# Attention's products with the values in plain float32, two groups of heads side by side in TensorE's column halves, and a seldom-run expert loop moved from the first pair of experts to the last

## The chip, the cores and the metric

One core of a Trainium2 chip runs the whole program. The metric is device time in microseconds (us), from the start to the end of one execution. The engines are TensorE (PE in the profile; its weight loads are PEld), VectorE (DVE), ScalarE (ACT), GpSimd (POOL) and SyncE (SP, which here issues nearly all transfers).

## The reference

512 tokens of width 1024 pass two blocks. The first block is one layer: a mixer of two attentions, then a mixture of experts. The second block is two layers of differential attention beside a Fourier mix, each followed by a SwiGLU.

```
# block 1, mixer: 8 heads of 64; "D" is top-k attention with one shared key/value head,
# "S", "W", "C" are selected, windowed and compressed attention with 2 key/value heads (4 query heads each)
p = masked_softmax(s, mask)
o = einsum('bthk,btkd->bthd', p, vs)
o_b = gc * o_cmp + gs * o_slc + gw * o_win
# block 1, experts: 32 experts, each token goes to 2 of them
y = (silu(gate) * up) @ w_down[e]
# block 2, per layer: 8 heads, values 64 wide, two score maps a head
p = softmax(s, axis=-1)
a = p[:, :, 0] - lam * p[:, :, 1]
o = einsum('bhqk,bkhd->bqhd', a, v)
```

All of it is float32.

## The kernel before

**Number formats.** Nearly every product of float32 matrices is made from three products of type float32r, a one-pass format with a shorter mantissa: each operand is split in a rounded high part and a low rest (`split`: a copy on ScalarE or VectorE, then a subtraction, usually on VectorE), and `mm3` adds high by high, high by low and low by high. The products of attention weights and values are made in another way. The values stand as a stationary tile of 128 columns, 64 of the high part and 64 of the low part (`VS` and `Vc` in block 1, `vs` in block 2); the attention weights `e` are split in `ph` and `pl`; two float32r matmuls of 512 columns then put the result of the high values into rows 0 to 63 of the bank `po` and that of the low values into rows 64 to 127. When a bank is complete, ScalarE copies its lower half (`pt`, `pot`) and VectorE adds the two halves (`o`, `op`).

The experts' products are plain float32: `up` and `down` work on a pair of experts, 64 slots each, and the two experts' results go to rows 0 to 63 and 64 to 127 of a bank, so that each matmul uses 64 of the array's 128 columns.

**Order of the work.** The program order on TensorE is made by generators. `weave` runs a chain (the attention's phases) against a fill (projections that do not depend on it) by a running estimate of TensorE's time, `self.pe`, which `mm` advances. `after` and `later` put work off by so many microseconds of that estimate. The instructions then pass the framework's scheduler, which may reorder an engine's instructions inside a stretch without branches.

**Block 1** (`attend1`). Units of work are a kind (S, W, C, then D) and one of four query blocks `i`. For each, `q_part` makes the sums of the softmax, `b_part` turns their logarithms into two more rows of the query operand, and `k_part` makes the scores again, transposed, with keys in the partitions, takes the exponential (`e`) and issues the products with the values. `k_part` goes over two groups of four heads `g`, and in each over the key blocks `j`. Each (g, j) puts one entry on the list `pend`; an entry is issued when more than four wait (`late`), or between the heads of the next `q_part`. There are 68 such entries: 20 for each of S, W and D, 8 for C.

**Block 2** (`mixer2`). `pv_phase` does the same for a pair of heads `j`: over the two heads `hd`, and in each over four key blocks `kt`, two score maps and exponentials `e0`, `e1`, their combination on VectorE, the split in `ph` and `pl`, and an entry on `pend`. There are 32 entries a layer. When a head pair is complete, `norm` follows, put off by `after`.

**Experts** (`experts`). A loop over pairs `p` of experts: `up`, `mid`, then for the pair before it `turn`, `down` and `scatter` (an add into the tokens' rows in memory by an indirect DMA). `chunk(c)` gathers the tokens of two pairs. The weights come in 192 units of 512 KB, which `fetch` requests when a buffer is freed; 31 buffers hold them. `rest_of_rows` serves the tokens of an expert beyond its 64 slots in a loop of dynamic length, `tc.For_i(0, n, 1)`, for which every engine loads the count `nblk` and all engines meet. With these inputs no expert has more than 64 tokens and the loop's body does not run. In the kernel before it stands in the pair p = 0:

```
            if not p:
                rest_of_rows()
            if prev:
                A = turn(prev[0], 128)
```

Of the kernel before, what the change touches and what calls it, by code (L numbers as in the profile page):

```python
# [32 lines left out]
T = 512  # L33
D = 1024
# [70 lines left out]
class Kernel:  # L105
# [374 lines left out]
    def mixer1(self, hT):  # L480
# [13 lines left out]
        VS = pers.tile([128, NT, 5, 128], F32R, name="VS")  # L494
# [13 lines left out]
        Vc = pers.tile([128, 2, 128], F32R, name="Vc")  # L508
        for z in (KAc, KCc, Vc):
            nc.vector.memset(z.bitcast(F32), 0.0)  # L510
# [138 lines left out]
        def proj_tok():  # L649

            raw = b1.tile([128, KT, 352], F32, name="vraw")
            hi = b1.tile([128, KT, 352], F32R, name="vhi")
            lo = b1.tile([128, KT, 352], F32R, tag="kraw", name="vlo")
            wv = w.rearrange("(k p) n -> p k n", p=128)
            for c, n, m in ((0, "va", 64), (64, "v_slc", 128), (192, "v_win", 128), (320, "wi", 8), (328, "gb", 24)):
                a = slice(c, c + m)
                nc.sync.dma_start(raw[:, :, a], wv[:, :, W_IN[n]:W_IN[n] + m])
                self.split(hi[:, :, a], lo[:, :, a], raw[:, :, a])
            for t in range(NT):
                ps = self.bank()  # L660
# [12 lines left out]
            nc.vector.scalar_tensor_tensor(e, lng, -1.0, lng, op0=OP.mult, op1=OP.max)  # L673
            nc.scalar.activation(e, e, AF.Exp, scale=-1.0)
            nc.vector.tensor_scalar(e, e, 1.0, None, op0=OP.add)
            le = b1.tile([128, NT, 24], F32, name="lgl")
            self.log(b1, le, e, "lgn")
            nc.vector.scalar_tensor_tensor(lng, lng, 0.0, le, op0=OP.min, op1=OP.subtract)
            bclose()
            self.mark("tok")  # L680

        def compress():
# [48 lines left out]
            for which in "kv":  # L731
# [28 lines left out]
                else:  # L760
# [3 lines left out]
                    nc.scalar.activation(Vc[0:31, :, 0:64], p, AF.Copy)  # L764
                    nc.vector.tensor_sub(Vc[0:31, :, 64:128], p, Vc[0:31, :, 0:64].bitcast(F32))
# [73 lines left out]
    def attend1(self, hT, DR, B, top_k, rt):  # L839
# [106 lines left out]
        def k_part(kind, i):  # L946
# [4 lines left out]
            for g in range(2):  # L951
                if first:
                    out[g] = self.bank("po")
                gs = slice(4 * g, 4 * g + 4)
                v = {"D": 0, "S": 1 + g, "W": 3 + g, "C": g}[kind]
                nj = 1 if kind == "C" else i + 1
                def pv(j, ph, pl, po=out[g], g=g, v=v):
                    st = B["Vc"][:, g] if kind == "C" else VS[:, j, v]
                    self.mm(po, st, ph, first and j == 0, False)
                    self.mm(po, st, pl, False, last and j == nj - 1)  # L960
                    if not last or j < nj - 1:
                        return
                    t = ap.tile([64, T], F32, tag="pt", name="pt")
                    nc.scalar.activation(t, po[64:128], AF.Copy)
                    o = ap.tile([128, 2, 128], F32, tag="o", name="o", bufs=2)
                    for r in range(2):
                        pick = lambda x: x.rearrange("p (a r t) -> p a r t", a=2, r=2)[:, :, r]
                        nc.vector.tensor_add(o[r * 64:(r + 1) * 64], pick(po[:64]), pick(t))
                    d = DR["oa" if kind == "D" else "ob"]
# [3 lines left out]
                for j in range(nj):  # L973
                    o = self.bank()
                    qa = QA[:, gs].rearrange("p h t -> p (h t)")
                    qb = QB[0:66, gs].rearrange("p h t -> p (h t)")
                    if kind == "C":
                        ka, kc = B["KAc"][:, g], B["KCc"][0:66, g]
                        mk = B["cmk"][:, i:i + 1].to_broadcast([128, 4, 128])
                    else:  # L980
                        js = slice(j * 128, (j + 1) * 128)
                        ka, kc = KA[:, v, js], KC[0:66, v, js]
                        mk = None
# [8 lines left out]
                    e = ap.tile([128, T], F32, tag="e", name="e", bufs=TUNE["ee"])  # L992
                    nc.scalar.activation(e, o, AF.Exp)
                    ph = ap.tile([128, T], F32R, tag="ph", name="ph", bufs=TUNE["eb"])
                    pl = ap.tile([128, T], F32R, tag="pl", name="pl", bufs=TUNE["eb"])
# [432 lines left out]
    def experts(self, R):  # L1428
# [133 lines left out]
        def rest_of_rows():  # L1562

            Xs, Y = (wp.tile([128, n], F32, name="rest", tag=f"rest{n}", bufs=1) for n in (KT * 64, D))
            wp.tile([128, 32], F32, name="gap", bufs=1)
# [4 lines left out]
            with tc.For_i(0, n, 1):  # L1570
# [15 lines left out]
                def unit(kind, k):  # L1586
                    raw = wp.tile([128, D], F32, tag="Y", name="Y", bufs=1)
# [11 lines left out]
        wp, wclose = self.pool("mw", 2, gap=104)  # L1599
# [16 lines left out]
        for p in range(17):  # L1616
# [205 lines left out]
    def mixer2(self, l, hT):  # L1822
# [35 lines left out]
        stacks, b8s, ops, puts, pend, tails = {}, {}, {}, [], [], []  # L1858

# [88 lines left out]
        def pv_phase(j):  # L1948
# [4 lines left out]
            def pv(po, hd, kt, ph, pl):  # L1953
                v = vs[:, kt, 2 * j + hd]
                self.mm(po, v, ph, kt == 0, False)
                self.mm(po, v, pl, False, kt == NT - 1)
                if kt == NT - 1:
                    if hd == 0:
                        while tails:
                            self.now(tails.pop(0))  # L1960
                        ops[j] = vp.tile([128, T], F32, tag="op", name="op", bufs=1)
                    t = vp.tile([128, T], F32, tag="po", name="pot", bufs=1)[:64]
                    nc.scalar.activation(t, po[64:128], AF.Copy)
                    nc.vector.tensor_add(ops[j][hd * 64:(hd + 1) * 64], po[:64], t)
                    if hd:
                        sq = vp.tile([128, T], F32, tag="sq", name="sq", bufs=1)
                        nc.scalar.activation(sq, ops[j], AF.Square)
                        tails.append(self.after(TUNE["sq"], lambda: norm(j, ops.pop(j), sq)))

            for hd in range(2):  # L1970
                po = self.bank("po")
                for kt in range(NT):
                    kk = slice(kt * 128, (kt + 1) * 128)
                    p = []
                    for c in range(2):
# [4 lines left out]
                        e = vp.tile([128, T], F32, tag=f"e{c}", name="e", bufs=TUNE["e2"])  # L1980
# [3 lines left out]
                    ph, pl = (vp.tile([128, T], F32R, tag=n, name=n, bufs=TUNE["p2"]) for n in ("ph", "pl"))  # L1984
                    self.split(ph, pl, p[0], (nc.scalar, nc.vector)[kt % 2], nc.gpsimd if kt % 2 < TUNE["pp"] else None)
                    pend.append(lambda a=(po, hd, kt, ph, pl): pv(*a))
                    yield
                    if len(pend) > TUNE["late2"]:
# [3 lines left out]
        def norm(j, op, sq):  # L1992
# [3 lines left out]
            v, c = (vp.tile([128, T], F32, tag=n, name=n, bufs=TUNE["e2"]) for n in ("e0", "e1"))  # L1996
# [14 lines left out]
        def proj_v(ws):  # L2011
# [11 lines left out]
            for t in range(NT):  # L2023
                p = ps[t].rearrange("p (h d) -> p h d", h=NH2)
                nc.scalar.activation(vs[:, t, :, 0:64], p, AF.Copy)
                nc.vector.tensor_sub(vs[:, t, :, 64:128], p, vs[:, t, :, 0:64].bitcast(F32))
# [64 lines left out]
        vs = vp.tile([128, NT, NH2, 128], F32R, name="vs", bufs=1)  # L2091
# [121 lines left out]
```

## Time and profile before

| | |
|---|---|
| median of 3 runs (lowest, highest) | 2066.06 us (2063.63, 2068.55) |
| the profiled execution, its own time | 2063.88 us |
| its span, first to last instruction | 2062.1 us |
| mean granted TensorE clock | 0.973 of full speed |
| busy in the span | PE 94%, PEld 74%, DVE 55%, ACT 41%, POOL 11% |

The stages, in us from the span's start: block 1's projections to about 190, its attention to about 430, merge and router to about 537, the experts to about 805; block 2's first layer has its attention from about 880 to 1050 and its SwiGLU until 1430, the second layer its attention from about 1490 to 1665. A busy time counts a matmul from start to modelled end, and matmuls overlap, so the spacing of their starts tells what one costs. In the window view each engine has its busy time and, in brackets, its number of instructions; PEclk is the granted clock (0.50 is 1.2 GHz, 1.00 is 2.4 GHz, a value between them a mixture of the two).

### The profile page before, as it was taken

How to read it: one execution, taken by the hardware profiler on the slowest of the kernel's cores; microseconds unless marked ns; L12 is line 12 of the kernel's file. 1: busy time of each engine (PE TensorE's matmuls, PEld its weight loads, DVE VectorE, ACT ScalarE, POOL GpSimd, SP SyncE). 2: the span in 40 equal slices, each digit the busy share in tenths (PEclk: the TensorE clock that was granted, in tenths of full speed). 3: DMA queues.
4: the chain of work that ended last, by engine and by line, in shares of the span. 5: the costliest groups of instructions: out<-in, count | busy, mean ns of one | idle time of the engine just before them, and what ended most of it. 6: DMA issues, size and time to landing. Idle time of an engine off the chain costs nothing.

```text
span 2062.1 us, 25783 instructions
## 1 busy us (share of the span) xinstructions
PE 1938.5 (94%) x9430; PEld 1519.1 (74%) x9430; DVE 1128.8 (55%) x2038; ACT 844.1 (41%) x1619; POOL 223.6 (11%) x186
## 2 busy tenths in 40 slices
PE   7689999999799999899999999999899999999998
PEld 6567778778555444777778888888687778888886
DVE  7687997654521213587884333234587983333234
ACT  5354656733212113576733323222476833323220
POOL 3143111033000101101010000001001010000001
PEclk9899999999899999999999999999999999999999
DMA  6666433377699996734424333433844335333332
GB/s 178 150 170 154 113 87 98 110 218 272 251 375 396 396 388 202 206 95 128 121 99 126 92 102 92 160 95 101 196 111 131 112 122 152 95 98 96 116 99 72
DMA packets 284496, 328.69 MB, mean 159 GB/s; under 512 B 25562, under 2 KB 206842, under 8 KB 284112
## 3 DMA queue, kind: packets, MB, share of 16 engines
q1 hardware_dynamic: 276912, 306.54, 47.7%
q0 software_dynamic: 7456, 20.49, 3.8%
q8 instruction: 75, 1.23, 0.2%
q14 instruction: 53, 0.43, 0.1%
HBM read 286.63 MB, written 43.38 MB: 160 GB/s over the span
## 4 chain that ended last, share of the span: by engine, by line
PE 49%; DVE 4%; DMA 3%; ACT 2%; issue 1%; SPq 0%; POOL 0%; POOLq 0%; DVEq 0%; ACTq 0%
PE b L136 46%; PE po L136 3%; DVE nm L1917 1%; DMA wr<-in_w_in_dram 1%; DMA ks<-bnc 1%; ACT b L1918 1%; DMA wr<-in_c_seq_dram 1%; PE tp L413 1%; DVE wl L245 0%; DMA wr<-in_w_o_dram 0%; DVE pl L245 0%; DMA qs<-bnc 0%; DVE e L1983 0%; ACT e L1981 0%; DMA bnc<-sl 0%
## 5 line engine op out<-in xcount | busy, mean ns | idle before, releaser
L136 PE MATMUL b<-hTh,wh 128*128 128x512 f32 (+1 forms) x1256 | 476.6, 381 | 6.3 <-ACT wh L242 3.8
L136 PE MATMUL b<-hTh,wl 128*128 128x512 f32 (+1 forms) x1256 | 472.0, 376 | 5.9 <-DVE wl L245 3.6
L136 PE MATMUL b<-hTl,wh 128*128 128x512 f32 (+1 forms) x1256 | 472.8, 377 | 1.1 <-DVE hTl L417 1.1
L242 ACT ACTIVATE wh<-wr 128x1024 fp32r<-128x1024 f32 (+1 forms) x217 | 220.6, 1020 | 568.5 <-PE b L136 341.7
L245 DVE TENSOR_TENSOR wl<-wr,wh 128x1024 fp32r<-128x1024 f32 (+1 forms) x207 | 255.4, 1234 | 338.9 <-ACT wh L242 338.5
L136 PEld LDWEIGHTS b<-hTh,wl 128*128 128x128 f32 x1256 | 240.4, 191 | 51.4 <-DVE wl L245 5.2
L136 PEld LDWEIGHTS b<-hTh,wh 128*128 128x128 f32 x1256 | 240.1, 192 | 49.1 <-ACT wh L242 4.6
L136 PEld LDWEIGHTS b<-hTl,wh 128*128 128x128 f32 x1256 | 240.7, 192 | 40.8 <-DVE hTl L417 3.2
L136 PE MATMUL b<-wl,ah 128*128 128x512 f32 x352 | 137.1, 390 | 0.0
L136 PE MATMUL b<-wh,ah 128*128 128x512 f32 x352 | 137.0, 389 | 0.0
L136 PE MATMUL b<-wh,al 128*128 128x512 f32 x352 | 136.9, 389 | 0.0
L396 POOL TENSOR_TENSOR rs_r<-rs_v,mhalf 128x1 f32<-128x1 f32 x20 | 26.7, 1333 | 780.9 <-DVE rs_v L392 780.9
L245 DVE TENSOR_TENSOR pl<-e,ph 128x512 fp32r<-128x512 f32 x132 | 99.4, 757 | 13.1 <-ACT ph L242 10.7
L1756 DVE TENSOR_TENSOR gs<-b,gs 128x512 f32<-128x512 f32 (+1 forms) x48 | 31.0, 647 | 137.6 <-PE b L136 137.5
L1918 ACT ACTIVATE b<-b,nm 128x512 f32<-128x512 f32 x128 | 84.8, 669 | 23.6 <-DVE nm L1917 23.2
L1917 DVE TENSOR_REDUCE nm<-b 128x1 f32<-128x512 f32 x128 | 82.5, 684 | 17.0 <-PE b L136 16.9
L245 POOL TENSOR_TENSOR wl<-wr,wh 128x1024 fp32r<-128x1024 f32 (+1 forms) x27 | 58.7, 2180 | 165.6 <-DVE wh L244 78.9
L136 PEld LDWEIGHTS b<-wh,al 128*128 128x128 f32 x352 | 66.1, 188 | 13.8
L136 PEld LDWEIGHTS b<-wh,ah 128*128 128x128 f32 x352 | 66.1, 188 | 13.7
L136 PEld LDWEIGHTS b<-wl,ah 128*128 128x128 f32 x352 | 66.1, 188 | 13.6
L1981 ACT ACTIVATE e<-b 128x512 f32<-128x512 f32 x128 | 70.8, 619 | 10.6 <-PE b L136 6.0
L1501 DVE SCALAR_TENSOR_TENSOR s<-b,sw,s 128x256 f32<-128x256 f32 x16 | 7.7, 484 | 119.0 <-ACT s L1500 118.9
(480 smaller groups left out, 3526.1 us busy)
## 6 DMA issues: line engine op xcount, KB each, us to landing
wr<-in_w_gu_dram SPq DMA_DIRECT2D x88, 512.0 KB, 3.8
xr<-in_w_gate_up_dram SPq DMA_DIRECT2D x61, 512.0 KB, 10.2
wr<-in_w_in_dram SPq DMA_DIRECT2D x60, 512.0 KB, 4.9
wr<-in_w_down_dram SPq DMA_DIRECT2D x44, 512.0 KB, 3.8
xw<-in_w_gate_up_dram SPq DMA_DIRECT2D x39, 512.0 KB, 11.3
xr<-in_w_down_dram SPq DMA_DIRECT2D x29, 512.0 KB, 10.9
xy<-in_w_gate_up_dram SPq DMA_DIRECT2D x28, 512.0 KB, 11.3
xw<-in_w_down_dram SPq DMA_DIRECT2D x21, 512.0 KB, 10.2
```

Source lines behind the costliest of these rows:

```text
L136: self.nc.tensor.matmul(out, a, b, start=start, stop=stop)
L242: nc.scalar.activation(hi, src, AF.Copy)
L245: (lo_eng or nc.vector).tensor_sub(lo, src, hi.bitcast(F32))
L396: nc.gpsimd.tensor_tensor(r, v, self.mhalf, op=OP.pow)
L413: nc.tensor.transpose(ps[:, j * 128:(j + 1) * 128], x[:, (f + j) * 128:(f + j + 1) * 128], self.ident)
L1501: nc.vector.scalar_tensor_tensor(s, ps[:m, 256:], w, s, op0=OP.mult, op1=OP.mult)
L1756: nc.vector.tensor_mul(g, ps, g)
L1917: nc.vector.tensor_reduce(nm[:, i, r:r + 1], ps, axis=AX.X, op=OP.max, negate=True)
L1918: nc.scalar.activation(ps, ps, AF.Exp, bias=nm[:, i, r:r + 1], accum_out=z[:, i, r:r + 1])
L1981: nc.scalar.activation(e, ps, AF.Exp)
```

## The change

Four things are done. (1) The values are kept as plain float32, 64 columns (`VS`, `Vc`, `vs`), and the attention weights are no longer split: `ph`, `pl`, `pt`, `pot` and their instructions are gone, and each former pair of float32r matmuls becomes one float32 matmul with a stationary tile of 64 columns. (2) Two groups share a bank: group or head 0 writes rows 0 to 63, group or head 1 rows 64 to 127, and the matmuls alternate between the halves. (3) The loops are turned inside out (key blocks outside, groups inside), an entry of `pend` now holds up to two key blocks of both halves (four matmuls), and an entry waits until one more is there. A full bank is moved out by two copies a group in block 1 (one on ScalarE, one on VectorE) and by one copy and one square of the bank in block 2. Buffers of `e` go from 3 to 9 (`e0` to 9, `e1` stays at 3). (4) `rest_of_rows` moves from p = 0 to p = 15, behind `turn`, and uses a buffer of the tag `X` for its tiles. In `mm` the estimate of a matmul with 64 stationary columns becomes half of that of another float32 matmul.

```diff
     def mm(self, out, a, b, start, stop):
         self.nc.tensor.matmul(out, a, b, start=start, stop=stop)
-        self.pe += b.free_size() * (0.425e-3 if b.dtype == F32R else 1.7e-3)
+        self.pe += b.free_size() * (0.425e-3 if b.dtype == F32R else 0.85e-3 if a.free_size() == 64 else 1.7e-3)
...
-        VS = pers.tile([128, NT, 5, 128], F32R, name="VS")
+        VS = pers.tile([128, NT, 5, 64], F32, name="VS")
...
-                nc.scalar.activation(VS[:, t, :, 0:64], p, AF.Copy)
-                nc.vector.tensor_sub(VS[:, t, :, 64:128], p, VS[:, t, :, 0:64].bitcast(F32))
+                nc.scalar.activation(VS[:, t], p, AF.Copy)
...
+            def pv(js, po=out[0]):
+                for j, es in js:
+                    for g, e in enumerate(es):
+                        st = B["Vc"][:, g] if kind == "C" else VS[:, j, v[g]]
+                        self.mm(po[g * 64:(g + 1) * 64], st, e, first and j == 0, last and j == nj - 1)
+                if not last or js[-1][0] < nj - 1:
+                    return
+                for g in range(2):
                     o = ap.tile([128, 2, 128], F32, tag="o", name="o", bufs=2)
                     for r in range(2):
+                        p = po[g * 64:(g + 1) * 64].rearrange("p (a r t) -> p a r t", a=2, r=2)[:, :, r]
+                        if r:
+                            nc.vector.tensor_copy(o[64:128], p)
+                        else:
+                            nc.scalar.activation(o[0:64], p, AF.Copy)
...
-                    self.split(ph, pl, e, (nc.scalar, nc.vector)[j % 2])
-                    pend.append(lambda pv=pv, a=(j, ph, pl): pv(*a))
+                    es.append(e)
                     yield
-                    if len(pend) > TUNE["late"]:
+                js.append((j, es))
+                if len(js) == 2 or j == nj - 1:
+                    pend.append(lambda pv=pv, js=js: pv(js))
+                    js = []
+                    if len(pend) > 1:
                         pend.pop(0)()
                         yield
...
-            if not p:
-                rest_of_rows()
             if prev:
                 A = turn(prev[0], 128)
+            if p == 15:
+                rest_of_rows()
...
+            def pv(po, kts):
+                for kt, ps in kts:
+                    for hd, p in enumerate(ps):
+                        self.mm(po[hd * 64:(hd + 1) * 64], vs[:, kt, 2 * j + hd], p, kt == 0, kt == NT - 1)
+                if kts[-1][0] == NT - 1:
+                    while tails:
+                        self.now(tails.pop(0))
+                    ops[j] = vp.tile([128, T], F32, tag="op", name="op", bufs=1)
+                    nc.vector.tensor_copy(ops[j], po)
+                    sq = vp.tile([128, T], F32, tag="sq", name="sq", bufs=1)
+                    nc.scalar.activation(sq, po, AF.Square)
```

## Rows read from the trace of the kernel before

**Rows 1.** Windows: busy time (instructions) of PE, PEld, DVE, ACT, POOL; clock; DMA.
```profile
200.00:300.00 100.00, 93.72 (x473) 77.59 (x472) 91.24 (x225) 63.97 (x151) 16.58 (x11) 0.95 0.45 111
...
1200.00:1300.00 100.00, 100.00 (x443) 82.81 (x442) 35.62 (x39) 29.23 (x38) 0.00 (x0) 1.00 0.33 95
```
**Rows 2.** PE's groups by line and form, whole span: busy, mean ns, idle before.
```profile
L136 PE MATMUL po<-ph,vs 128*128 128x512 f32 x64 | 27.0, 421 | 1.7 <-ACT ph L242 1.7
...
L136 PE MATMUL po<-ph,VS 128*128 128x512 f32 x60 | 26.3, 442 | 0.5 <-DVE ph L244 0.5
L136 PE MATMUL po<-pl,VS 128*128 128x512 f32 x60 | 26.0, 434 | 5.8 <-DVE pl L245 5.8
L136 PE MATMUL po<-pl,vs 128*128 128x512 f32 x64 | 25.6, 400 | 2.0 <-DVE pl L245 2.0
```
**Rows 3.** Timeline of PE, block 2's attention: start, length, instruction.
```profile
919.40 0.39 PE L136 MATMUL po<-ph,vs 128*128 128x512 f32 x1
919.63 0.40 PE L136 MATMUL po<-pl,vs 128*128 128x512 f32 x1
```
**Rows 4.** Timeline of PE, experts' stage.
```profile
650.15 0.64 PE L136 MATMUL b<-S,H2l 128*128 128x256 f32 x4
650.72 3.65 PE L136 MATMUL b<-xw,A 128*64 128x512 f32 x16
654.20 5.32 PE L136 MATMUL b<-xw,X 128*64 128x512 f32 x24
659.35 1.89 PE L136 MATMUL b<-xy,X 128*64 128x512 f32 x8
661.17 0.50 PE L1508 MATMUL b<-ident,s 128*128 128x128 f32 x2
```
**Rows 5.** Timeline of PE weight loads, experts' stage.
```profile
651.63 0.14 PEld L136 LDWEIGHTS b<-xw,A 128*64 128x64 f32 x2 [0.28 <-issue]
```
**Rows 6.** Timeline of PE, late in the experts' stage.
```profile
762.52 1.02 PE L136 MATMUL b<-xr,X 128*64 128x512 f32 x2
763.47 0.74 PE L136 MATMUL b<-S,H2h 128*128 128x256 f32 x4
```
**Rows 7.** DVE's groups by line and form, 175 to 450 us.
```profile
L245 DVE TENSOR_TENSOR pl<-e,ph 128x512 fp32r<-128x512 f32 x68 | 51.3, 760 | 10.0 <-ACT ph L242 8.3 <-PE b L136 0.3
...
L244 DVE CAST ph<-e 128x512 fp32r<-128x512 f32 x24 | 11.9, 494 | 3.2 <-PE po L136 2.8 <-ACT e L993 0.3
```
**Rows 8.** Timeline, end of block 1's attention; in brackets the idle time before.
```profile
415.73 6.02 DVE L245 TENSOR_TENSOR pl<-e,ph 128x512 fp32r<-128x512 f32 x3
...
421.80 0.80 PE L136 MATMUL po<-pl,VS 128*128 128x512 f32 x1 [3.68 <-DVE pl L245]
...
427.94 0.67 PE L136 MATMUL b<-t,wh 128*128 128x512 f32 x2
```
**Rows 9.** Waits of PE, 175 to 450 us: total, times, longest.
```profile
PE b L136 <- ACT b L926: 3.1, 4, 1.5
...
PE b L136 <- DVE b L876: 2.7, 1, 2.7
```
**Rows 10.** Timeline of PE around the loop at p = 0.
```profile
545.20 1.05 PE L136 MATMUL b<-V,S 128*128 128x6 f32 x8
556.62 1.22 PE L136 MATMUL b<-S,H2h 128*128 128x256 f32 x4 [10.36 <-issue]
```
**Rows 11.** Timeline of DVE around the loop at p = 0.
```profile
548.15 0.87 DVE L1422 SCALAR_TENSOR_TENSOR S<-iota,pc,S 128x256 fp32r<-128x256 f32 x2
...
550.58 0.17 DVE L1481 CAST ix<-sw 128x2 int32<-128x2 f32 x1
```
**Rows 12.** Window of 10 us at the loop, columns as in Rows 1.
```profile
550.00:560.00 10.00, 3.38 (x16) 3.38 (x17) 0.96 (x5) 0.00 (x0) 0.00 (x0) 0.50 0.32 127
```
**Rows 13.** Timeline of ACT and DVE at the last pair.
```profile
795.79 0.38 ACT L1500 ACTIVATE s<-b 128x256 f32<-128x256 f32 x1 [7.84 <-PE b L136]
...
796.21 0.48 DVE L1501 SCALAR_TENSOR_TENSOR s<-b,sw,s 128x256 f32<-128x256 f32 x1 [8.39 <-ACT s L1500]
```

More of the change, by code (lines that the diff above doesn't have):

```diff
@@ L507, in mixer1 @@
         KCc = pers.tile([128, 2, 128], F32R, name="KCc")
-        Vc = pers.tile([128, 2, 128], F32R, name="Vc")
-        for z in (KAc, KCc, Vc):
-            nc.vector.memset(z.bitcast(F32), 0.0)
+        Vc = pers.tile([128, 2, 64], F32, name="Vc")
+        for z in (KAc.bitcast(F32), KCc.bitcast(F32), Vc):
+            nc.vector.memset(z, 0.0)
         nc.gpsimd.memset(KC.bitcast(F32)[64:128], 0.0)
@@ L950, in k_part @@
             first, last = kind in "DS", kind in "DC"
[L951 to L964, printed above, removed]
+            if first:
+                out[0] = self.bank("po")
@@ new lines, in k_part @@
+            nj = 1 if kind == "C" else i + 1
+            v = {"D": (0, 0), "S": (1, 2), "W": (3, 4), "C": (0, 1)}[kind]
+            def pv(js, po=out[0]):
[5 more added lines that the diff above has]
+                    return
+                d = DR["oa" if kind == "D" else "ob"]
+                for g in range(2):
@@ L970, in pv @@
                     nc.sync.dma_start(d[g * 256:(g + 1) * 256, i * 128:(i + 1) * 128].rearrange("(a p) t -> p a t", p=128), o)
                     made[kind == "D"] += 1
-                for j in range(nj):
+            js = []
+            for j in range(nj):
+                es = []
+                for g in range(2):
                     o = self.bank()
+                    gs = slice(4 * g, 4 * g + 4)
                     qa = QA[:, gs].rearrange("p h t -> p (h t)")
                     qb = QB[0:66, gs].rearrange("p h t -> p (h t)")
+                    mk = None
@@ L1562, in rest_of_rows @@
         def rest_of_rows():
-            Xs, Y = (wp.tile([128, n], F32, name="rest", tag=f"rest{n}", bufs=1) for n in (KT * 64, D))
-            wp.tile([128, 32], F32, name="gap", bufs=1)
+            flat = wp.tile([128, 2560], F32, tag="X", name="flat")
+            Xs, Y = flat[:, :512], flat[:, 1536:]
             blk = mp.tile([128, 1], F32, name="blk")
@@ L1586, in unit @@
                 def unit(kind, k):
-                    raw = wp.tile([128, D], F32, tag="Y", name="Y", bufs=1)
+                    raw = flat[:, 512:1536]
                     nc.sync.dma_start(raw, self.unit_src(kind, e, k))
@@ L1598, in experts @@
         next(first)
-        wp, wclose = self.pool("mw", 2, gap=104)
+        wp, wclose = self.pool("mw", 2, gap=72)
         self.run(first)
@@ L1951, in pv_phase @@
             qs, ks = stacks.pop(j)
[L1953 to L1973, printed above, removed]
+            def pv(po, kts):
[9 more added lines that the diff above has]
+                    nc.scalar.activation(sq, po, AF.Square)
+                    tails.append(self.after(TUNE["sq"], lambda: norm(j, ops.pop(j), sq)))
+            po, kts = self.bank("po"), []
+            for kt in range(NT):
+                kk = slice(kt * 128, (kt + 1) * 128)
+                both = []
+                for hd in range(2):
                     p = []
@@ L1979, in pv_phase @@
                         self.mm(ps[:, kk], self.identr, dg[:, 2 * j + hd], False, True)
-                        e = vp.tile([128, T], F32, tag=f"e{c}", name="e", bufs=TUNE["e2"])
+                        e = vp.tile([128, T], F32, tag=f"e{c}", name="e", bufs=EB[c])
                         nc.scalar.activation(e, ps, AF.Exp)
@@ L1983, in pv_phase @@
                     nc.vector.scalar_tensor_tensor(p[0], p[1], nlam, p[0], op0=OP.mult, op1=OP.add)
-                    ph, pl = (vp.tile([128, T], F32R, tag=n, name=n, bufs=TUNE["p2"]) for n in ("ph", "pl"))
-                    self.split(ph, pl, p[0], (nc.scalar, nc.vector)[kt % 2], nc.gpsimd if kt % 2 < TUNE["pp"] else None)
-                    pend.append(lambda a=(po, hd, kt, ph, pl): pv(*a))
+                    both.append(p[0])
                     yield
-                    if len(pend) > TUNE["late2"]:
+                kts.append((kt, both))
+                if len(kts) == 2:
+                    pend.append(lambda kts=kts: pv(po, kts))
+                    kts = []
+                    if len(pend) > 1:
                         pend.pop(0)()
@@ L1994, in norm @@
             self.mm(ps, ones2, sq, True, True)
-            v, c = (vp.tile([128, T], F32, tag=n, name=n, bufs=TUNE["e2"]) for n in ("e0", "e1"))
+            v, c = (vp.tile([128, T], F32, tag=f"e{n}", name=f"e{n}", bufs=EB[n]) for n in range(2))
             eng = nc.vector if j == 3 else nc.gpsimd
@@ L2090, in mixer2 @@
         vp, vclose = self.pool("m2v", 2)
-        vs = vp.tile([128, NT, NH2, 128], F32R, name="vs", bufs=1)
+        vs = vp.tile([128, NT, NH2, 64], F32, name="vs", bufs=1)
         M = self.fourier_weights(l, vp)
```

20 lines of the change are left out of this document (7 added, 13 removed).

## The prediction

> **What bounds the kernel now.** I read the windows of 100 us first. In the dense stages (SwiGLU, 1200 to 1300 us) PE is busy all the time at full clock while VectorE and ScalarE do a third of a window; in block 1's attention PE has 6 us in a hundred without work and a clock of 0.95, and VectorE is at 91 [rows 1]. So PE sets the time everywhere, and in the attention stages it also loses some to waits and to the lower clock that follows them. A gain must therefore be PE's: fewer or denser matmuls, shorter waits, or less half clock. VectorE's and ScalarE's work is worth something only where PE waits for it. Then I read PE's groups for what the products with the values cost and wait for [rows 2], the timeline for the spacing of matmuls [rows 3], the experts' stage, where the before has the form of matmul that the change brings [rows 4 to 6], and last the surroundings of the loop [rows 10 to 13].
>
> **Matmuls.** There are 132 entries, 68 in block 1 and 64 in block 2. Each has two float32r matmuls of 512 columns; 248 of the 264 are in [rows 2], the 16 others are the same form against `Vc`. One costs the distance to the next start, 0.23 us [rows 3]: 264 x 0.23 = 60.7 us go. A plain float32 matmul leaves two records each: the experts' 512 records of `up` and 256 of `down` are twice the number of calls. In a run of alternating halves a record takes (659.35 - 654.20) / 24 = 0.2146 us [rows 4], a matmul 0.43. So 132 x 0.43 = 56.7 us come, and the term is **-4.0 us**. The upper bound is a matmul whose partner in the other half isn't beside it: two records alone take 763.47 - 762.52 = 0.95 us [rows 6], 0.85 without the change of form priced next. All 132 alone would be 112 us. I take the paired price, since the code issues the halves in turn and an entry's inputs are one entry old when it is issued, so that neither should be late.
>
> **Changes of form.** Before and behind a run of half-width matmuls the starts show a gap. The four gathers that start at 650.15 are spaced by 0.12 and would end at 650.63; the first half-width one starts at 650.72: 0.09 us. Behind, eight records from 659.35 would end at 661.07; the transposition starts at 661.17: 0.10 us [rows 4]. The new entries are 38 runs: 22 in block 1 (six each for S, W, D, as one, one, two and two entries for the four query blocks; four for C) and 16 in block 2. 38 x 0.19 = **+7.2 us**. Lower bound 0, if entries lie next to each other; upper bound about 15, if the scheduler cuts each in two.
>
> The row shows a cost of 0.19 us for a run; the Trainium skill, TensorEngine Tiling (Array Packing), Key Properties, says that switching the tiling mode drains TensorE, and the trace agrees. It gives no figure, so the sum is the same with it; the rule speaks against the change.
>
> Matmuls and changes of form together, -4.0 + 7.2, cost PE 3 us more than before.
>
> **Waits of the products.** PE stood idle before these matmuls for 1.7 + 0.5 + 5.8 + 2.0 = 10.0 us, for `ph` or `pl` [rows 2]. The longest shows the price of what follows: 3.68 us idle at 421.80, behind three `pl` that took 6 us where one takes 0.76 [rows 7, 8], and then 14 matmuls in 427.94 - 421.80 = 6.14 us, at half clock; at 0.23 they take 3.2, so 2.9 more were lost. The other low-clock stretches behind such waits I estimate at as much again, 3 us. Together 16 us. The new matmul waits for `e` only, in block 2 for the combined `e`: two steps, rounding and subtraction, fall out of the chain. At the end of an attention, where nothing is left to fill with, PE will still wait for the exponential. I count three quarters: **-12 us**. Bounds: 0 and -16.
>
> **Relief of the other engines.** In block 1's attention VectorE loses 51.3 + 11.9 us of its busy time [rows 7], more than a quarter of what it does there, and the other 44 of the 68 roundings leave ScalarE. What can gain by it are PE's waits for the softmax sums, 3.1 us on ScalarE's exponentials and 2.7 us on the bias row [rows 9]. Waits of this kind in block 2's two layers I put at 4 us each, half clock behind all of them at 5: 19 us, of which I count a third, as the load falls by a quarter and queues by more: **-6 us**. Bounds 0 and -13. The new copies out of a bank replace a copy and additions of the same size or smaller and are counted as nothing; what hides them is that the next bank is free, and one bank fewer is held.
>
> **The loop.** At p = 0 PE's last matmul before it starts at 545.20 and ends its group about 546.2; the next starts at 556.62, 10.4 us idle [rows 10]. Then the clock is 0.50 until 560 [rows 12] and, I estimate, for another microsecond: 4.4 us at half rate, 2.2 lost. Of these 12.6 us something remains: the choice matrix of the next chunk needs VectorE until 549.0 [rows 11], up to 2.8 us unless `up` of the second pair goes first. So 11 us gained. The weights' stream had a hole at the same place, its share of the DMA engines at 0.32 [rows 12], and loses it too, so it can keep up with the earlier start. At p = 15 the loop stands behind `up` of the last pair. ScalarE starts its part of `s` at 795.79, when PE has filled the bank, and VectorE ends its part at 796.69 [rows 13]: with the release some 1.2 us behind PE. In the loop at p = 0 the stretch from VectorE's last instruction, 550.75, to PE's next was 5.9 us [rows 10, 11]. So 7.1 us idle and 2 us of half clock: 9 lost, since `down` of two pairs and the sums wait behind it on PE, and the loads of the tokens' rows behind it on SP. Between the loop and their use PE has 32 records of `down`, 6.9 us at the spacing above, and three groups of transpositions, so I count the loads as hidden. Term **-2 us**. Bounds: -12 (nothing lost at the end) and +9 (nothing gained at the start).
>
> **Sum.** -4.0 + 7.2 - 12 - 6 - 2 = -16.8 us. The profiled execution took 2063.9 us on its own; that gives 2047, and as the median of the runs is 2.2 us above it, I forecast 2049 us, with a range of its own of 2041 to 2057.
>
> **Rivals.**
>
> *The waits only change their name.* PE then waits for `e` as long as it did for `pl`, and VectorE's and ScalarE's relief isn't where PE waits; an exponential comes two steps earlier only where nothing else queues ahead of it. With a fifth of these two terms the sum is -4 + 7.2 - 3 - 1 - 2 = -3, or 2063 us: no change that can be measured. For it: the attention window loses only 6 us [rows 1]. Against it: 6.6 us (3.68 and 2.9) sit in one place, whose cause goes.
>
> *The halves do not run side by side.* One mechanism, in the products with the values: where the scheduler or a late `e` separates the two halves, a matmul costs 0.85 instead of 0.43. It happens in the before, late in the experts' stage [rows 6], where the two inputs come at different times. All 132 so: +56 us, 2105 us. It turns the sign at some 40 of the 132. Against it: the inputs of an entry are old, and most of the experts' records are paired [rows 4].
>
> *Weight loads in the open.* If a weight load ran only while no matmul did, 264 loads of 0.14 us [rows 5] would add 36 us: 2085 us. In the experts' stage loads of this size are there every 0.43 us and the records still follow at 0.2146 [rows 4, 5], so the loads are hidden there. The Trainium skill, TensorE: Matmul & The Clock Gate, Part 3, What overlaps and what doesn't, says that a load overlaps running matmuls only where its row group differs; by it the two halves, which use all rows, would give this time. The trace doesn't agree.
>
> *The loop costs at both ends.* If the early start is eaten by the weights' stream, the loop's term is +9 and the time 2060 us.
>
> **Numbers.** Forecast 0.55, waits that change name 0.17, separated halves 0.13, loads in the open 0.02, loop 0.11, and 0.02 for something slower that I do not see. A measurement of this kernel can tell 0.2%, 4 us, from no change. The loop's case lies at that border and is split, 0.07 faster and 0.04 the same. Faster 0.62, the same 0.21, slower 0.17. The range is 2036 to 2069: the low end takes the larger bounds of the waits and of the relief, the high end leaves out most of the separated halves and of the loads in the open.
>
> **What would show it.** The half-width matmuls on `po` should start in pairs a few ns apart, a pair of records every 0.43 us; a lone record every 0.43 us is the second rival. Gaps of 0.09 and 0.10 us around each run. PE's idle time before `po` should fall from 10 us to 3 or less, and the half clock behind 421.80 be gone. VectorE's share in 200 to 300 us should fall from 91 to about 70. At 546 us PE should go on within 3 us, and a gap of about 7 us should stand before the last pair's `down`. Wrong would be the forecast if the scheduler, given other lengths, orders the fill work worse, so that waits for transfers grow, or if the order of the experts' stage changes.

## The result, and the profile after

The changed kernel takes 2037.39 us (median of 4 runs, 2033.61 to 2040.41), the kernel before on the same chip 2067.31 us (4 runs): ratio 0.9856, 95% interval 0.9837 to 0.9874, 29.9 us faster. The forecast was 2049 us with a range from 2036 to 2069. The direction was right, the time lies in the range near its low end, and the gain is almost twice the 17 us of the sum.

The profiled execution took 2040.41 us (span 2038.6, mean clock 0.981). Its marks against those of before: the products with the values of block 1 end at 396.2 us instead of 421.8, the experts start at 519.0 instead of 538.2, their last `up` or `down` starts at 780.8 instead of 803.3, and block 2's last matmuls with `ah` at 2028.4 instead of 2051.9. So most of the gain is there before the experts start. (Some 6 us of it seem to be lost between the products and the experts. But from the first matmul of `w_out` to the experts' start the profile of before takes 69.5 us, the one of after 73.6, and those of loop_alone and block2_alone below, whose work there is that of before, 73.9 and 76.4. So it is the profile of before that was short there, and not that of after that was long.)

The windows of block 1's attention, before (the two that follow the first line of [rows 1]):

```profile
300.00:400.00 100.00, 93.13 (x474) 76.16 (x473) 75.06 (x184) 65.34 (x178) 11.96 (x8) 0.95 0.39 109
400.00:422.00 22.00, 17.75 (x80) 13.52 (x79) 18.29 (x27) 15.68 (x27) 7.97 (x9) 0.98 0.33 81
```

and after:

```profile
200.00:300.00 100.00, 99.83 (x527) 71.87 (x526) 77.53 (x198) 55.45 (x152) 16.24 (x11) 1.00 0.46 121
300.00:397.00 97.00, 96.78 (x501) 70.31 (x500) 53.99 (x137) 58.90 (x159) 15.20 (x13) 1.00 0.40 110
```

Two losses can be read from such a row. PE's idle time is the length less the busy time: before 6.3 + 6.9 + 4.3 = 17.4 us, after 0.4. The clock is the second: a stretch of length T at a mean clock c does at most (1 - c) x T less work than at full clock; before that is 5 + 5 + 0.4 = 10.4 us, after nothing. Together 27.4 us are gone, and the products end 25.6 us earlier.

PE's groups, answering [rows 2]: the idle time before the products fell from 10.0 us to 0.4, all of it at the tail of block 2's attention.

```profile
L136 PE MATMUL po<-e,vs 128*64 128x512 f32 x128 | 32.8, 605 | 0.4 <-DVE e L1989 0.4
...
L136 PE MATMUL po<-e,VS 128*64 128x512 f32 x120 | 30.6, 607 | 0.0
```

An entry in block 2's attention on the timeline of PE, answering [rows 3]:

```profile
1508.17 0.22 PE L136 MATMUL b<-dg,identr 128*128 128x128 f32 x1
1508.23 0.45 PE L136 MATMUL b<-qs,ks 128*128 128x512 f32 x1
1508.52 0.22 PE L136 MATMUL b<-dg,identr 128*128 128x128 f32 x1
1508.67 1.94 PE L136 MATMUL po<-e,vs 128*64 128x512 f32 x8
1510.54 0.50 PE L136 MATMUL b<-qs,ks 128*128 128x512 f32 x1
```

and two of its weight loads, which lie under the matmuls that start at the same time:

```profile
1509.15 0.14 PEld L136 LDWEIGHTS po<-e,vs 128*64 128x64 f32 x2 [0.29 <-issue]
```

A matmul of 128 columns takes 0.06 (1508.17 to 1508.23), so the run could have started at 1508.58: 0.09 us in front. Behind, 1510.54 - 1508.67 = 1.87 us, where 8 records at 0.2146 [rows 4] make 1.72: 0.15. A change of form and back costs 0.24 to 0.25 us, not 0.19: besides the 0.10 behind, the first pair of records keeps the array some 0.05 us longer than the others.

Waits of PE in block 1's attention, 200 to 397 us, answering [rows 9] (total, times, longest); this is all that is left:

```profile
PE b L136 <- ACT b L925: 0.4, 2, 0.2
```

Waits of PE in the experts' stage, 505 to 785 us, answering [rows 10]: the 10.4 us of the loop at p = 0 are gone, and the loop at p = 15 (the line with DVEq) costs 2.1 us, with no half clock behind it.

```profile
PE b L136 <- DVE S L1429: 3.1, 2, 2.0
PE b L1692 <- DVEq L1577: 2.1, 1, 2.1
PE b L136 <- ACT A L1517: 0.5, 1, 0.5
```

But the stage from its first to its last `up` or `down` is only 3.3 us shorter (261.8 for 265.1). On PE's timeline one sees why:

```profile
681.18 0.63 PE L136 MATMUL b<-S,H2h 128*128 128x256 f32 x4
681.74 1.07 PE L136 MATMUL b<-xy,X 128*64 128x512 f32 x2
682.75 0.74 PE L136 MATMUL b<-S,H2l 128*128 128x256 f32 x4
```

Two records alone take 1.0 us, as in [rows 6]. Counting the half-width records of the stage that have no other within 60 ns, 40 are lone in the kernel before and 68 in the one after; there are 92 changes of form instead of 82. A lone record takes 0.43 instead of 0.2146, so 28 x 0.21 + 5 x 0.25 = 7 us are lost by the order of `up`, `down` and the gathers.

### The profile page after: what moved, and what is told of

Read it like the earlier page. It is cut to its first block, busy times and chain, and to the rows that moved or that the text cites. A ratio compares the mean times of both kernels' runs of the same rounds, so it can differ in the third digit from the quotient of the medians.

```text
span 2038.6 us, 25300 instructions
## 1 busy us (share of the span) xinstructions
PE 1937.3 (95%) x9430; PEld 1477.4 (72%) x9430; DVE 1013.3 (50%) x1813; ACT 787.2 (39%) x1528; POOL 224.2 (11%) x186
## 4 chain that ended last, share of the span: by engine, by line
PE 53%; DVE 3%; DMA 2%; ACT 2%; issue 1%; POOL 0%; SPq 0%; POOLq 0%; ACTq 0%; DVEq 0%
PE b L136 49%; PE po L136 3%; DMA ks<-bnc 1%; DVE nm L1925 1%; ACT b L1926 1%; PE tp L414 1%; DMA bnc<-sl 0%; DMA gcol<-in_subln_g_dram 0%; DVE op L2014 0%; DVE e L1989 0%; DVE wl L246 0%; DVE hTl L418 0%; PE b L1949 0%; DMA bnc<-sh 0%; DVE x L1727 0%
## 5 line engine op out<-in xcount | busy, mean ns | idle before, releaser
L136 PE MATMUL b<-ks,qs 128*128 128x512 f32 x128 | 56.0, 460 | 15.2 <-DMA ks<-bnc 8.9
```

## The experiments

Times are medians, ratios are against the kernel before on the same chip.

**The parts one by one.** Each part of the diff alone on the kernel before, and the whole without the loop's move.

```diff
# loop_alone: kernel before with this and the loop's new tiles (tag X)
-            if not p:
-                rest_of_rows()
             if prev:
                 A = turn(prev[0], 128)
+            if p == 15:
+                rest_of_rows()
# loop_back: changed kernel with these lines and the loop's tiles as in the kernel before
# block1_alone: only the hunks of VS, Vc, k_part and mm;  block2_alone: only those of vs, pv_phase, norm and mm
```

> The kernel before with the loop moved to p = 15 and nothing else. Forecast's term: -2 us. Theory from the comparison of the two traces (the loop is worth about 12 us at p = 0, loses about 2.5 at p = 15, and some 5 go to a finer interleaving of `up` and `down` late in the stage, because the instructions are no longer cut into two stretches at p = 0): -4 to -6 us, with lone half-width records from about 690 us on. Rival (the interleaving comes from block 1's shorter attention, since the weights' stream then starts later against the experts): about -10 us.

> The kernel before with the new products in block 1 alone; loop at p = 0, block 2 as before. By the forecast's terms, block 1's share is about -9 us (matmuls -2, forms +4, waits -8.5, relief -2.5). By the comparison of the traces it is -19 to -21: the attention ends 26 earlier, and some 6 of them are lost again in the merge because the projections beside it end only 20 earlier.

> The kernel before with the new products in block 2 alone. By the forecast's terms about -6 us in both layers together (matmuls -2, forms +3, waits -3.5, relief -3.5). By the comparison of the traces between -3 and +2: the largest waits of these stages are for transfers of `ks` and stay.

> The changed kernel with the loop back at p = 0 (and its own buffers as before). Against the kernel before: if the parts add up, the changed kernel's -30 us without the loop's own worth, so -24 to -26 by the theory from the traces, -28 by the forecast's -2, -20 by the rival's -10. PE idle about 10 us at the loop again.

| | median, us | ratio, 95% | gain, us |
|---|---|---|---|
| loop_alone | 2063.92 | 0.9985 (0.9975 to 0.9995) | 2 to 3 |
| block1_alone | 2041.81 | 0.9887 (0.9870 to 0.9904) | 23 to 24 |
| block2_alone | 2060.39 | 0.9972 (0.9961 to 0.9983) | 5 to 6 |
| loop_back | 2037.39 | 0.9856 (0.9841 to 0.9872) | 28 to 30 |

(The gain is given by the medians and by the ratio.) Block 1 makes the gain, above either expectation. Block 2 gives what the forecast's terms said; the comparison of the two traces alone, which had put it near nothing, was wrong. Its windows show it: before, 880 to 1044 and 1486 to 1658 us,

```profile
880.00:1044.00 164.00, 153.40 (x755) 125.15 (x754) 138.11 (x221) 119.78 (x250) 10.77 (x10) 0.97 0.41 112
1486.00:1658.00 172.00, 160.17 (x795) 130.33 (x794) 143.47 (x233) 124.93 (x263) 10.78 (x10) 0.99 0.41 113
```

and in block2_alone, from the same starts to the ends of the attentions there:

```profile
880.00:1036.00 156.00, 148.84 (x743) 112.82 (x743) 109.69 (x165) 105.35 (x226) 10.91 (x10) 0.99 0.42 114
1486.00:1650.00 164.00, 154.37 (x765) 117.23 (x765) 111.05 (x172) 108.17 (x233) 11.37 (x10) 0.99 0.40 111
```

Idle time and clock together fall from 10.6 + 4.9 + 11.8 + 1.7 = 29 us to 7.2 + 1.6 + 9.6 + 1.6 = 20. (42 fewer of PE's records lie in the second pair of windows, so their lengths alone are no measure.) In the changed kernel itself, where block 1 ends earlier, the same stages lose 5.8 + 4.7 + 10.5 + 1.7 = 22.7, so there the fall is 6 us and not 9:

```profile
856.00:1014.00 158.00, 152.24 (x748) 116.11 (x746) 104.95 (x159) 102.28 (x217) 11.09 (x10) 0.97 0.40 113
1461.00:1631.00 170.00, 159.46 (x789) 121.01 (x788) 115.45 (x177) 112.31 (x243) 11.37 (x10) 0.99 0.39 111
```

The loop's move is worth 2 to 3 us alone and nothing beside the new products (loop_back is as fast as the changed kernel). With the loop at p = 0 the stage has 40 lone records and 82 changes in the kernels that have it there (before, block1_alone, block2_alone, loop_back), and in loop_alone 52 and 92. So the finer order comes with the move, as the first theory had it, and not with block 1's shorter attention; how many records it leaves alone differs with the rest.

**Block 1: load or wait?** Load kept does the splits again without using them. Wait kept also makes the products wait for them. No low leaves out the subtraction alone, in the kernel before (the products then count `ph` twice, which changes the numbers but not the count of PE's records). Bank held was meant to take one bank more out of use.

```diff
# load_kept: changed kernel, behind the exponential of block 1
+                    ph = ap.tile([128, T], F32R, tag="ph", name="ph", bufs=2)
+                    pl = ap.tile([128, T], F32R, tag="pl", name="pl", bufs=2)
+                    self.split(ph, pl, e, (nc.scalar, nc.vector)[j % 2])
# wait_kept: the rounding to ph likewise, and instead of the subtraction
+                    nc.vector.tensor_tensor(e, e, ph.bitcast(F32), op=OP.max)
# no_low: kernel before, the split replaced by its rounding
-                    pend.append(lambda pv=pv, a=(j, ph, pl): pv(*a))
+                    pend.append(lambda pv=pv, a=(j, ph, ph): pv(*a))
# bank_held: changed kernel, per unit; a second memset stands in the program where the unit's bank is complete
+                out[1] = self.bank("ph")
+                nc.vector.memset(out[1][:, 0:1], 0.0)
```

> The changed kernel, but in block 1 the rounding and the subtraction are still done for every `e`, on the same engines as before, and nobody reads what they make. It has the new products without the relief of VectorE and ScalarE in block 1. Block 1's part gained 24 us by itself, where the forecast had 9. Theory A (the size was missed in the relief: the softmax sums, masks and copies of the stage queue behind the splits): 12 to 18 us slower than the changed kernel, 2050 to 2056 us. Rival B (it was missed in the products' own wait, which falls away here too): 0 to 4 us slower, 2037 to 2041.

> The changed kernel, but in block 1 each `e` is rounded to `ph` as before and then replaced in place by the larger of `e` and `ph` on VectorE (instead of the subtraction), so that the products wait for both steps as before (the attention weights are then off by the rounding). Load as in load kept, and the wait too. Rival B: some 8 to 12 us slower than load kept, 2056 to 2060, with PE idle before `po` again. If the products' inputs are old enough with the new entries even so: as load kept, 2046 to 2050, and the products' wait was removed by the later issue, not by the shorter chain.

> The kernel before, with block 1's subtraction left out and the rounded part `ph` used in both of a product's matmuls (the low part of the attention weights is left out of block 1's result). PE's matmuls and the rounding step stay, VectorE loses 51 of the 63 us that the whole change takes from it. Theory A: 10 to 16 us faster than before, 2050 to 2056. Rival B: most of the waits on `pl` go (8.1 us of idle time in the whole kernel, about 6 of them here) with the half clock behind them, 6 to 9 us faster, 2057 to 2060. The forecast's relief term alone would be 2 us.

> The changed kernel, but in block 1 every unit holds a second bank, as the kernel before did for its second group: the bank is marked by two short memsets on VectorE, at the unit's start and end, and nobody computes with it. Load kept cost about 11 of block 1's 24 us. Theory C (most of the rest is the bank that the change sets free: the waits on banks that the softmax sums still read, ScalarE's and VectorE's, were 3.1 and 2.7 us in the kernel before with half clock behind them): 6 to 12 us slower than the changed kernel, 2043 to 2049. Rival B (the rest is the products' own wait for the split): 0 to 3 us slower.

| | median, us | ratio, 95% | against the change's 0.9856, of 2066 us |
|---|---|---|---|
| load_kept | 2048.24 | 0.9916 (0.9899 to 0.9933) | +12 |
| wait_kept | 2065.73 | 0.9992 (0.9977 to 1.0006) | +28 |
| no_low | 2060.14 | 0.9969 (0.9957 to 0.9982) | (6 faster than before) |
| bank_held | 2037.74 | 0.9858 (0.9840 to 0.9877) | 0 |

Load kept lies at the low end of theory A (11 us slower by the medians, 12 by the ratios): the load is about half of block 1's gain. Its windows and waits of PE in block 1's attention:

```profile
200.00:300.00 100.00, 97.25 (x503) 68.90 (x501) 94.43 (x229) 61.11 (x156) 16.48 (x11) 1.00 0.41 107
300.00:408.00 108.00, 104.73 (x512) 74.84 (x512) 83.50 (x187) 73.79 (x194) 15.26 (x12) 0.97 0.37 103
```

```profile
PE b L136 <- ACT b L925: 5.5, 8, 1.5
PE b L136 <- DVE o L969: 0.2, 1, 0.2
```

VectorE is at 94 of 100 again, PE waits for the softmax sums' exponentials on ScalarE (L925, the line that was L926 in [rows 9]) and loses 6.0 us idle and 3.2 by the clock; 18 of block 1's 136 records of the products are lone instead of 4, 14 x 0.21 = 3 us. That makes the 12.

Wait kept loses the rest and is as slow as the kernel before. Its waits of PE between 200 and 427 us, and two entries of two matmuls each on its timeline:

```profile
PE po L136 <- DVE e L1005: 14.5, 13, 4.3
```

```profile
298.46 1.08 PE L136 MATMUL po<-e,Vc 128*64 128x512 f32 x4
...
303.70 1.75 PE L136 MATMUL po<-e,VS 128*64 128x512 f32 x4 [0.49 <-DVE e L1005]
```

The first entry is paired: 4 records in 1.08 us. In the second the two inputs came one after the other, and the same work took 1.75. 64 of block 1's 136 records are lone. Against load kept that is 9.1 us more idle, 46 x 0.21 = 9.8 us more by lone records, and 3.2 less by the clock: 15.7 us, as the ratios say (28 - 12 = 16). So this form of matmul bears a late input badly, and the entries' longer wait in the list alone does not make the inputs old. But it does not price the wait in the kernel before, whose matmuls use all columns and have no partner to miss: 10 of the 16 us are a loss that only the new form has.

No low gained 5 to 6 us, at the low end of B and far from A. The wait for the split all but went, and others stayed:

```profile
PE b L136 <- DMA QA<-d_qa: 4.6, 1, 4.6
PE b L136 <- ACT b L926: 3.4, 7, 0.9
PE b L136 <- DVE b L876: 3.3, 1, 3.3
...
PE po L136 <- ACT ph L998: 0.4, 1, 0.4
PE po L136 <- DVE ph L996: 0.2, 1, 0.2
```

Before `po` 0.6 us are left of 6.5, yet PE's clock is still 0.95 and 0.97 and its idle time 13.3 us (it was 17.4):

```profile
200.00:300.00 100.00, 94.80 (x484) 79.49 (x482) 78.86 (x202) 65.09 (x154) 16.32 (x11) 0.95 0.44 111
300.00:414.00 114.00, 105.89 (x546) 87.54 (x545) 65.22 (x167) 78.60 (x200) 15.88 (x13) 0.97 0.38 104
```

In the changed kernel and in load kept the waits for `QA` and on L876 do not occur, although load kept has the full load. Which part of the change removes them (the new order of issue, the larger number of buffers of `e`, the bank set free) wasn't told apart. Bank held does not settle the bank, because it did not hold one. Its two memsets of one unit on VectorE's timeline:

```profile
356.51 0.06 DVE L953 MEMSET ph<- 128x1 f32 x1
356.64 0.06 DVE L966 MEMSET ph<- 128x1 f32 x1
```

They lie 0.13 us apart in six of the eight units, 0.39 and 2.1 us in the other two. The second depends on the first alone and not on the unit's products, and in the trace it stands right behind it; this unit's own bank is moved out only from 369.64 on. So the second bank was free again at once, and theory C is left untested.

**The array's two halves.**

```diff
# halves_apart: changed kernel, both blocks; here block 2
-                for kt, ps in kts:
-                    for hd, p in enumerate(ps):
+                for hd in range(2):
+                    for kt, ps in kts:
# single_blocks: changed kernel, both blocks
-                if len(js) == 2 or j == nj - 1:
+                if True:
-                    if len(pend) > 1:
+                    if len(pend) > 2:
```

> The changed kernel with the matmuls of an entry ordered by half instead of alternating, in both blocks: in the 28 entries of two key blocks the order of the halves is 0, 0, 1, 1. If a matmul whose neighbour is in its own half costs 0.85 us and not 0.43, an entry of four takes 2.6 us (only the two in the middle side by side) to 3.4 us instead of 1.7: 24 to 48 us slower, 2061 to 2085. If the two halves gain nothing from alternating (the spacing is one of the single matmul): no change.

> The changed kernel with entries of one key block (two matmuls) instead of two, and one more entry kept waiting, so that the inputs are about as old: 66 runs of half-width matmuls instead of 38, both blocks. At 0.09 + 0.10 us a run, 28 x 0.19 = 5.3 us slower, 2043; if a change of form is hidden beside other work, no change.

Halves apart: 2039.76 us, ratio 0.9872 (0.9852 to 0.9892), which overlaps the change's interval, and no 24 us. An entry on its timeline, whose instructions stand in the order half 0, 0, 1, 1:

```profile
1508.56 1.94 PE L136 MATMUL po<-e,vs 128*64 128x512 f32 x8
1510.43 0.50 PE L136 MATMUL b<-qs,ks 128*128 128x512 f32 x1
```

The eight records take 1.87 us to the next start, as in the alternating order. In the trace the records of such runs still start in pairs, 12 to 14 ns apart instead of 6 or 7. The trace does not record the half of a matmul, but this gap is a sign that the scheduler kept the new order: runs of four records, for which both orders are the same, still have 6 or 7 ns. Read so, a matmul of half 1 starts while one of half 0, issued before it, is still waiting for its turn. What keeps the halves side by side is then that both have work at hand, not that it alternates.

Single blocks: 2053.65 us, ratio 0.9945 (0.9928 to 0.9962), 16 to 18 us slower than the changed kernel where 5.3 were expected. A run of two matmuls:

```profile
1520.63 1.08 PE L136 MATMUL po<-e,vs 128*64 128x512 f32 x4
1521.64 0.50 PE L136 MATMUL b<-hTh,wh 128*128 128x512 f32 x1
```

1.01 us for 4 records, 0.15 more than 4 x 0.2146, as above. The trace has 62 runs where the changed kernel has 36; 26 x 0.25 = 6.5 us. The other 10 are not in the products (4 lone records in block 1, as in the changed kernel): the other order of the fill work brings waits back, among them 2.4 us on L925 and 2.4 on the squares in front of `norm`. They weren't priced one by one.

**The loop.**

```diff
# loop_mid8: changed kernel with the buffers of loop_back and
-            if p == 15:
+            if p == 8:
                 rest_of_rows()
# no_loop: changed kernel without the call
```

> The changed kernel with the loop in the pair p = 8, behind `turn`, with the buffers of the kernel before. Theory: the loop cuts the instructions into two stretches and the order of `up` and `down` starts afresh behind it; in the program 58 changes into and out of half-width matmuls are left in the stage, where the changed kernel has 98 and the kernel before 88. So lone records almost vanish (68 in the changed kernel, worth 0.21 us each against paired ones, and 40 x 0.1 us of changes): 6 to 12 us gained, the loop in the middle costs 2 us (as at p = 15) to 12 (as at p = 0). Together -8 to +2 against the changed kernel, 2029 to 2039.

> The changed kernel without the loop (tokens beyond an expert's 64 slots are left out; there are none with these inputs). What the loop still costs at p = 15: 2.1 us of idle time and half a microsecond after it, so 2 to 3 us faster than the changed kernel. Rival (a barrier there costs more than its idle time shows, by loads behind it): 6 us or more. The finer interleaving of `up` and `down` stays in the program (96 changes against 98).

Loop mid8: 2044.38 us, ratio 0.9887 (0.9871 to 0.9903), 6 us slower than the changed kernel. The order did start afresh: 4 lone records and 52 changes. But PE was idle at the loop for 22.5 us. Waits of PE in the stage, and windows at the loop:

```profile
PE b L136 <- DMA xr<-in_w_gate_up_dram: 22.5, 1, 22.5
```

```profile
640.00:650.00 10.00, 7.70 (x37) 2.69 (x36) 3.97 (x19) 0.77 (x2) 1.55 (x1) 1.00 1.03 380
650.00:660.00 10.00, 0.00 (x0) 0.00 (x0) 0.00 (x0) 0.00 (x0) 0.00 (x0) 0.61 1.03 409
660.00:670.00 10.00, 0.00 (x0) 0.00 (x0) 0.00 (x0) 0.00 (x0) 0.00 (x0) 0.50 0.58 232
670.00:680.00 10.00, 9.82 (x48) 7.66 (x50) 0.24 (x2) 2.06 (x5) 0.00 (x0) 0.70 0.05 7
```

All engines stand still while the transfers go on at full share, and until the stream has run dry (0.05 behind the loop). The timeline of VectorE there names what ended its wait:

```profile
670.11 0.24 DVE L1553 TENSOR_SCALAR pc<-pos 128x8 f32<-128x8 f32 x2 [21.87 <-DMA xr<-in_w_gate_up_dram]
```

SP has weight loads to issue in front of the loop, nine of them after VectorE's last instruction ended at 648.24:

```profile
656.92 2.89 SPq L1226 DMA_DIRECT2D xr<-in_w_gate_up_dram  x3
```

It is done with them at 659.8 us, and the last piece of the last one lands at 669.59, half a microsecond before the engines go on. In the kernel before, at p = 0, the same line of VectorE:

```profile
556.51 0.24 DVE L1546 TENSOR_SCALAR pc<-pos 128x8 f32<-128x8 f32 x2 [5.76 <-DMA xr<-in_w_gate_up_dram]
```

There the last pieces of the three loads still under way land at 553.08, 554.35 and 555.61, and the engines' semaphore instructions of the loop go on at 553.09, 554.37 and 555.62. So in these runs the engines go on behind the loop's entry only when every load under way has landed. At p = 15 the weights have all come (the last piece at 761.52), the last scatter has landed at 768.39, before VectorE ends its own work at 770.69, and PE goes on at 771.89. That loop mid8 is only 6 us slower fits the prices found above: against the changed kernel it has 20.4 us more idle time there and loses 3.0 by the clock behind it (0.70 in 670 to 680), and 64 fewer lone records and 40 fewer changes give 13.4 + 5.0 back.

No loop: 2036.39 us, ratio 0.9857 (0.9839 to 0.9875): no difference from the changed kernel. Its experts' stage is 4 us shorter (257.8), but the measurement does not show them in the whole.

## Why the direction was right and the size was not

**Matmuls**, -4.0: right but for 12 lone records, 4 of 136 in block 1 and 8 of 128 at the ends of block 2's attentions, which give back 2.5 us. Records follow in pairs at the expected spacing, also with the halves' order changed; the rival of weight loads in the open is out, since a pair's loads lie under the matmuls here too. (The rule of the Trainium skill that was weighed in the forecast, TensorE: Matmul & The Clock Gate, Part 3, What overlaps and what doesn't, isn't borne out here either: loads of 136 ns, and a pair of records still every 0.43 us.)

**Changes of form**, +7.2: right in kind, somewhat small. 36 runs x 0.25 = +9 us; the price left out the longer first pair.

**Waits of the products**, -12, and **Relief of the other engines**, -6: the step that failed, by size. The two lost some 27 us in block 1 and 6 to 9 in block 2, where 18 were counted in all. The working took a wait's price from its idle time and from half clock behind one wait, and put the rest at a few microseconds. But [rows 1] already had the whole loss: a clock of 0.95 in a window of 100 us is up to 5 us beside the 6 idle ones, and so 11 in this hundred, and with the two windows that follow it 28 in block 1's attention, of which the change left 0.4. "The attention window loses only 6 us" was the misreading, and it stood in favour of the rival that the waits only change their name. The relief in block 1 alone is 12 us (load kept), twice the term for both blocks and near its bound of 13: 9 of the 27 us of idle time and clock, and 3 by lone records. The other 18 go with what else the change does there: the shorter chain, the new order of issue with more buffers of `e`, the bank set free. How much of it each is worth is not shown. Three quarters of the one term and a third of the other were shares without a row behind them. Block 2's 5 to 6 us were right, with idle time and clock 9 us down in block2_alone against some 3 us more for matmuls, forms and lone records.

**The loop**, -2: the number was right by itself (2 to 3), but by luck, since two errors cancel in its working. The 5.9 us from VectorE's last instruction to PE's next at p = 0 were taken as the price of the meeting; they are weight loads landing, and at p = 15, where none is under way, the stretch takes 1.2. So the loss at the end was 2.1 us idle without half clock, where 9 were counted. What took the gain back is the finer order of the experts, some 4 us in loop_alone (12 lone records and 10 changes more) and 7 in the changed kernel, which the forecast named only as what would make it wrong.

Parts and whole: -4 + 2.5 + 9 - 27, -6 to -9 for block 2 and 0 to -3 for the loop make -25.5 to -31.5; measured were -29.9.

Of the rivals, "the waits only change their name" did not happen: waits on `b` fell with those before `po`. "The halves do not run side by side" cost little here, since 12 of 264 records are lone; wait kept shows when it would cost more. "The loop costs at both ends" did not happen. Of the signs, pairs, idle time before `po` and the missing half clock came as named; VectorE's share in 200 to 300 us fell to 77.5, not to 70, as more of the stage now fits in the window; the gap before the last pair's `down` was 2.1 us, not 7.

## What to carry to other kernels

Price a stage's waits from the window as idle time plus (1 - clock) x length, before sharing them out among causes: in block 1 both went with the waits. Half-width plain float32 matmuls are a fair exchange for two fp32r ones when their inputs are old, since a late one costs the idle time and the pairing as well. Put a loop of dynamic length where no transfers are under way, and look at what order the scheduler makes of the work around its new place.

## What was not expected of the hardware

The two column halves seem to work as streams of their own: in halves apart the order 0, 0, 1, 1 ran as fast as 0, 1, 0, 1. The Trainium skill, TensorEngine Tiling (Array Packing), Key Properties, says that tiles operate independently and that different tiles can load weights and multiply in parallel; the trace agrees (1.87 us for eight records in both orders).

The same loop, not entered, cost PE 10.4, 2.1 or 22.5 us idle by its place, mostly through the loads under way at its entry (5.9 of the 10.4 us, nearly all of the 22.5).

Idle time and clock do not go together in a fixed ratio: wait kept was idle for 15.1 us in block 1's attention, longest 4.3, at a clock of 1.00, load kept for 6.0 us with 0.97 in its second window.
